# The roots of six late norms go through DRAM to reach all partitions, where TensorE transposed them before

## The chip, the cores and the metric

The kernel runs on one NeuronCore of a Trainium2 chip. The metric is the device time of one execution in microseconds (us). The program is scheduled ahead of time: each engine (TensorE = PE, VectorE = DVE, ScalarE = ACT, GpSimd = POOL, and SyncE = SP, which issues nearly all DMAs) has one fixed list of instructions, runs it in order, and waits at an instruction until what it needs is there.

## The reference

One layer over 2048 frames of 1024 features, in float32. Both sub-layers sit between two RMS norms:

```
def rms_norm(x, g):
    y = x * rsqrt(mean(x * x, axis=-1) + RMS_EPS)
    return y * g

h = rms_norm(x, g_pre_mix)
m = chunk_relpos_attention(h, w_qkv, w_o, rel_bias)      # 16 heads, 64-frame chunks, 8 chunks back
x = x + rms_norm(m, g_post_mix)
h = rms_norm(x, g_pre_ffn)
x = x + rms_norm((silu(h @ w_gate) * (h @ w_up)) @ w_down, g_post_ffn)   # 2816 hidden features
```

A norm needs one number per frame, the root 1/sqrt(mean + eps).

## The kernel before, in words

Data lie features on partitions, frames along the row: a tile of 128 partitions x 512 frames is one block of features of a half of 512 frames. Four halves make two groups (g = 0 and 1) of 1024 frames. Attention for both groups comes first, then, for each group, `gate_up(g)` and `down(g)`. Matrix products are made as three float32r matmuls of high and low parts (`products`, lines 192 to 194), 512 columns each. The feed-forward products are cut into seven products per block (Strassen's scheme): `gate_up` has 11 chunks, each of which does the products B11, B21 (into bank pair `pa`), T1 (`pc`), T2 (`pb`), B22 (`pc` again), T3 and T4 (`pb` again), 24 matmuls each. Between them DVE and ACT read the banks: line 1017 copies, 1031 and 1032 make the differences and sums `u2` and `p5` after T1 and T2, 1036 closes, 1047 makes the outputs T1 to T4, which SP stores to DRAM. T3 adds into the banks that line 1031 has to have read. Weights come by DMA into one of four `raw` buffers; ACT (line 128) rounds them to a high part and DVE (line 129) forms the low part.

The work of the norms is laid beside those products as a list of small steps, `later`. Every three matmuls one unit of credit (`tick`) is given, and a step is put into the program when its price is paid; `pause(w)` is a step that only costs w. PE's list is in the order in which this is written. The lists of the other engines and of the SP queue are put in order by a scheduler that works with estimated times, so an instruction of theirs can stand well before or after the place at which its step was written.

A late norm goes like this. `Late.sums` loads eight tiles and adds their squares into `total` (128 partitions x 512 frames, each partition with its own sums). `rstd_steps` then has `by_token`: four matmuls against a column of ones give the sums over partitions as a 128 x 4 column (frame on partition; line 275), DVE scales it (280), POOL raises it to the power -1/2 (282) into `rs`. After a pause of 6, `back` needs that root as a row, the same in every partition: `transposed` (line 302) lets PE multiply the column, repeated 128 times, with the identity, four times 128x128, and ACT (297) copies the bank over `total`. `Late.write` then loads y and the residual again, multiplies by `total` (line 1212), adds (1215) and stores.

There are four such norms: two after the mixing of group 1 during `gate_up(0)`, two after the feed-forward of group 0 during `gate_up(1)`. Besides, `blocks[1]` (the norm ahead of group 1's feed-forward) sums its two halves during `gate_up(0)`, keeps the roots as columns `hr`, and `spreads` makes two rows `row` of them; line 795 reads these when `blocks[1].all` makes the operands of `gate_up(1)`.

Of the kernel before, what the change touches and what calls it, by code (L numbers as in the profile page):

```python
# [9 lines left out]
F32 = mybir.dt.float32  # L10
# [6 lines left out]
P = 128  # L17
# [6 lines left out]
HALF = 512  # L24
# [26 lines left out]
def trunk(  # L51
# [22 lines left out]
    dram = ctx.enter_context(tc.tile_pool(name="dram", bufs=1, space=DRAM))  # L74
# [123 lines left out]
    later = deque()  # L198
# [29 lines left out]
    def pause(w):  # L228
        return [(w, lambda: None)]
# [27 lines left out]
        act.activation(sq, src, AF.Square)  # L257
        eng.tensor_tensor(total, total, sq, op=ALU.add)

    def rstd_steps(total, dst, wait=8.0, keep=None, bank=None, extra=None, then=None):  # L260

        nb = total.shape[-1] // P
        bank = bank or norm_bank
        r = {}

        def by_token():  # L270
            pt = bank("pssq")
            for b in range(nb):
                terms = [total] if extra is None else [total, extra]
                for n, t in enumerate(terms):
                    pe.matmul(  # L275
                        pt[:, 0, b : b + 1], t[:, b * P : b * P + P], ones[:, 0:1],
                        start=n == 0, stop=n == len(terms) - 1,
                    )
            m = const.tile([P, 4], F32, tag="ms", name="ms", bufs=2)
            dve.tensor_scalar(m[:, :nb], pt[:, 0, :nb], 1.0 / D, EPS, op0=ALU.mult, op1=ALU.add)  # L280
            r[0] = const.tile([P, 4], F32, tag="rs", name="rs", bufs=2) if keep is None else keep
            pool.tensor_tensor(r[0][:, :nb], m[:, :nb], neg_half.to_broadcast([P, nb]), op=ALU.pow)  # L282

        def back():
            if then is None:
                spread(r[0], dst, bank)
            else:
                then(transposed(r[0], nb, bank))

        return [(1.0, by_token)] + pause(wait) + [(1.0, back)]  # L290

    def norm_bank(name):
# [2 lines left out]
    def spread(r, dst, bank=norm_bank):  # L295

        act.activation(dst, transposed(r, dst.shape[-1] // P, bank), AF.Copy)

    def transposed(r, nb, bank):
        pt = bank("prs")  # L300
        for b in range(nb):
            pe.transpose(pt[:, b, :], r[:, b : b + 1].to_broadcast([P, P]), ident)
        return pt[:, :nb, :].rearrange("p b t -> p (b t)")

    class Prep:
# [26 lines left out]
        def rstd(self, wait=8.0, bank=None):  # L332
            return [(0.0, lambda: later.extendleft(reversed(rstd_steps(self.total, self.r, wait, bank=bank))))]
# [62 lines left out]
    class Post:  # L396
# [11 lines left out]
        def rstd(self, wait=8.0):  # L408
            return rstd_steps(self.total, self.total, wait)
# [37 lines left out]
    phase = {}  # L447
# [304 lines left out]
    class Blocks:  # L752
# [9 lines left out]
        def sums(self, w):  # L762

            steps = []
            for t in range(2):
                c = {}

                def load(k, t=t, c=c):
                    c[k] = io("sum")
                    sp.dma_start(c[k], self.src[t][:, k, :])  # L770

                def use(k, c=c):
                    if k == 0:
                        self.total = nrm_tile("total")
                    add_square(c.pop(k), self.total, k == 0)

                steps += behind(w, KT, 1, load, use)
                steps.append((3.0, lambda t=t: rstd_steps(self.total, None, keep=self.r[t])[0][1]()))
            return steps

        def spreads(self):
            self.rows = []

            def one(t):
                row = phase["fp"].tile([P, HALF], F32, tag="tot", name="row", bufs=2)
                self.rows.append(row)
                spread(self.r[t], row)

            return [(1.0, lambda t=t: one(t)) for t in range(2)]

        def column(self, dst, t, k):
            sp.dma_start(dst, self.src[t][:, k, :])

# [191 lines left out]
    def bank(name):  # L985
        return phase["psf"].tile([P, HALF], F32, tag="pd", name=name, bufs=6)
# [192 lines left out]
    class Late:  # L1179
# [17 lines left out]
            return behind(w, KT, 1, load, use)  # L1197

        def rstd(self, wait):
            return [(0.0, lambda: later.extendleft(reversed(rstd_steps(self.total, self.total, wait))))]  # L1200

        def write(self, w):
            c = {}
# [17 lines left out]
    def begin():  # L1221
# [28 lines left out]
        for k in range(KT):  # L1250
            if k % 2 == 0:
                c, here = k // 4, slice(k % 4 * 256, k % 4 * 256 + 512)
                sp.dma_start(raws[c][:, here], plan[0][:, k * 256 : k * 256 + 512])
                hi, lo = ready[0][c]
                split_part(hi[:, here], lo[:, here], raws[c][:, here])
            column(0, k, cols[0][k])
# [4 lines left out]
        for k in range(KT):  # L1261
            column(1, k, cols[1][k])
# [67 lines left out]
    def dense():  # L1330
# [57 lines left out]
        for g in range(NG):  # L1388
            i = 2 * g
            if g == 0:  # L1390
                later.extend(blocks[0].third(1.5) + pause(44.0))
                for t in range(2):
                    late = Late(y_d[t], POST_MIX, x[2 + t], x1_d[2 + t])
                    later.extend(late.sums(6.0) + late.rstd(6.0) + late.write(10.0))
                later.extend(pause(12.0) + blocks[1].sums(8.0) + blocks[1].spreads())
            else:
                for late in halves:
                    later.extend(late.sums(6.0) + late.rstd(6.0) + late.write(10.0))
# [19 lines left out]
            total, begun, last_sq, rows_ = [], set(), {}, [None, None]  # L1418
# [70 lines left out]
    blocks = [Blocks(g) for g in range(NG)]  # L1489
# [7 lines left out]

    sums = weight_sums()
    work = dense()
    spent = [0.0]  # L1500
    owed = [0.0]
# [26 lines left out]
    for g in range(NG):  # L1528
# [4 lines left out]
        due, total = [], 0.0  # L1533
# [99 lines left out]
```

## Time and profile before

| | us |
|---|---|
| median of 3 timed runs | 2411.97 (2411.55 to 2414.48) |
| the profiled execution | 2410.04 |
| its span, first to last instruction | 2408.2 |
| PE busy | 2390.0 |
| DVE busy | 1459.0 |
| ACT busy | 1030.7 |
| POOL busy | 295.0 |

The span is what lies between the first and the last instruction; 1.8 us of the profiled execution lie outside it. An engine's busy time is the time in which its records show an instruction in work; PE's are pipelined, so their ends are modelled, and the starts tell the pace. `gate_up(0)` runs from about 1062 to 1484 us, `down(0)` to about 1760, `gate_up(1)` to about 2080, `down(1)` to the end.

### The profile page before, as it was taken

To read this page: it belongs to the slowest core of one execution; us is meant where nothing else is said; L and a number is where in the kernel's file an instruction comes from. 1 tells how busy PE (TensorE), PEld (TensorE's weight loads), DVE (VectorE), ACT (ScalarE), POOL (GpSimd) and SP (SyncE) were. 2 spreads that over 40 slices of the span, in tenths; PEclk is the share of its full clock that TensorE was granted. 3 is DMA by queue.
4 is the path that set the end of the run, shared out by engine and by line. 5 is a ranking of instruction groups with operands and counts; after the bars stand their busy time and mean duration, and the time that the engine had idled before them with its cause. 6 is when DMAs were issued, how large, how long until landed. Compare 5 with 4: busy or idle time off the path is not lost.

```text
span 2408.2 us, 34848 instructions
## 1 busy us (share of the span) xinstructions
PE 2390.0 (99%) x12562; PEld 1991.2 (83%) x12562; DVE 1459.0 (61%) x2568; ACT 1030.7 (43%) x1805; POOL 295.0 (12%) x382
## 2 busy tenths in 40 slices
PE   9999999999999999999999999999999999999998
PEld 8888888789787878878888888888888888888886
DVE  6546465586555554666666665577656755555577
ACT  5344344554344443545333343365443333334454
POOL 0233332102233322210000000000000000000002
PEclk9999999999999999999999999999999999999999
DMA  7689988757988875555576663577667754457654
GB/s 220 182 215 241 256 233 222 233 178 203 228 239 228 229 182 127 158 178 194 172 260 204 229 201 123 174 229 257 214 211 244 232 172 155 141 173 236 193 192 153
DMA packets 195836, 488.41 MB, mean 203 GB/s; under 512 B 25392, under 2 KB 27456, under 8 KB 185936
## 3 DMA queue, kind: packets, MB, share of 16 engines
q1 hardware_dynamic: 190032, 451.59, 58.6%
q0 software_dynamic: 5632, 34.61, 8.5%
q8 instruction: 99, 1.62, 0.3%
q14 instruction: 73, 0.60, 0.1%
HBM read 356.54 MB, written 148.42 MB: 210 GB/s over the span
## 4 chain that ended last, share of the span: by engine, by line
PE 56%; DVE 0%; POOL 0%; issue 0%; ACT 0%; DVEq 0%
PE pd L193 6%; PE pd L192 6%; PE pd L194 6%; PE pb L192 5%; PE pb L193 5%; PE pb L194 5%; PE pa L192 3%; PE pc L192 3%; PE pa L193 3%; PE pa L194 3%; PE pc L193 3%; PE pc L194 3%; PE mm L192 1%; PE mm L193 1%; PE mm L194 1%; PE pssq L275 0%
## 5 line engine op out<-in xcount | busy, mean ns | idle before, releaser
L596 ACT ACTIVATE sc<-sc,nmax 128x640 f32<-128x640 f32 (+4 forms) x256 | 193.1, 756 | 250.8 <-DVE nmax L592 250.5
L192 PE MATMUL mm<-hb,whi 128*128 128x512 f32 x704 | 283.7, 403 | 0.5 <-ACT y L253 0.5
L194 PE MATMUL mm<-hb,wlo 128*128 128x512 f32 x704 | 276.3, 392 | 0.0
L193 PE MATMUL mm<-hb,whi 128*128 128x512 f32 x704 | 275.5, 391 | 0.0
L600 POOL TENSOR_SCALAR sc<-sc,rows 128x640 f32<-128x640 f32 (+4 forms) x256 | 191.4, 750 | 644.1 <-DVE rows L599 618.2
L592 DVE CUSTOM_DVE_ANT_0 sc<-st,bias 128x640 f32<-128x640 f32 (+4 forms) x256 | 179.4, 737 | 73.1 <-PE st L584 71.4
L192 PE MATMUL pb<-hb,whi_gu_T 128*128 128x512 f32 x528 | 206.0, 390 | 0.0
L194 PE MATMUL pb<-hb,wlo_gu_T 128*128 128x512 f32 x528 | 205.5, 389 | 0.0
L193 PE MATMUL pb<-hb,whi_gu_T 128*128 128x512 f32 x528 | 205.4, 389 | 0.0
L282 POOL TENSOR_TENSOR rs<-ms,neg_half 128x4 f32<-128x4 f32 (+1 forms) x11 | 17.0, 1547 | 1234.2 <-DVE ms L280 1234.2
L194 PEld LDWEIGHTS mm<-hb,wlo 128*128 128x128 f32 x704 | 132.1, 188 | 28.9
L192 PEld LDWEIGHTS mm<-hb,whi 128*128 128x128 f32 x704 | 132.5, 188 | 24.5 <-issue 1.6
L193 PEld LDWEIGHTS mm<-hb,whi 128*128 128x128 f32 x704 | 132.6, 188 | 21.8
L193 PE MATMUL pd<-a,whi_d_T 128*128 128x512 f32 (+1 forms) x368 | 140.0, 380 | 0.4 <-DVE a L376 0.4
L192 PE MATMUL pd<-a,whi_d_T 128*128 128x512 f32 (+1 forms) x368 | 140.1, 381 | 0.0
L194 PE MATMUL pd<-a,wlo_d_T 128*128 128x512 f32 (+1 forms) x368 | 139.7, 380 | 0.0
L583 PE MATMUL st<-k,q 128*128 128x384 f32 (+1 forms) x448 | 137.9, 329 | 0.0
L192 PE MATMUL pa<-hb,whi_gu_B 128*128 128x512 f32 x352 | 137.3, 390 | 0.0
L194 PE MATMUL pa<-hb,wlo_gu_B 128*128 128x512 f32 x352 | 137.0, 389 | 0.0
L193 PE MATMUL pa<-hb,whi_gu_B 128*128 128x512 f32 x352 | 137.0, 389 | 0.0
L129 DVE TENSOR_TENSOR wlo_gu_T<-raw,whi_gu_T 128x1024 fp32r<-128x1024 f32 x88 | 107.5, 1221 | 48.2 <-ACT whi_gu_T L128 48.0
L128 ACT ACTIVATE whi_gu_T<-raw 128x1024 fp32r<-128x1024 f32 x88 | 93.2, 1060 | 91.3 <-PE pa L193 29.0
(230 smaller groups left out, 5666.2 us busy)
## 6 DMA issues: line engine op xcount, KB each, us to landing
raw<-gu_S SPq DMA_DIRECT2D x88, 512.0 KB, 3.7
raw<-in_w_gu SPq DMA_DIRECT2D x66, 512.0 KB, 4.0
q<-stage SPq DMA_DIRECT2D x128, 256.0 KB, 5.8
y<-y SPq DMA_DIRECT2D x96, 256.0 KB, 4.3
gu_S<-in_w_gu SPq DMA_DIRECT2D x44, 512.0 KB, 6.3
raw_d<-d_S SPq DMA_DIRECT2D x88, 256.0 KB, 3.6
raw_a<-aT SPq DMA_DIRECT2D x88, 256.0 KB, 3.7
raw<-in_w_a SPq DMA_DIRECT2D x42, 512.0 KB, 6.4
```

The costliest lines, as they stand in the source:

```text
L128: act.activation(hi, raw, AF.Copy)
L129: dve.tensor_tensor(lo, raw, hi.bitcast(F32), op=ALU.subtract)
L192: pe.matmul(pt, a_hi, b_hi, start=first, stop=False, skip_group_check=go_on)
L193: pe.matmul(pt, a_hi, b_lo, start=False, stop=False, skip_group_check=go_on)
L194: pe.matmul(pt, a_lo, b_hi, start=False, stop=last, skip_group_check=go_on)
L282: pool.tensor_tensor(r[0][:, :nb], m[:, :nb], neg_half.to_broadcast([P, nb]), op=ALU.pow)
L583: pe.matmul(st[:, a:b], q[:, 2 * h, cols], kk[:, h, key], start=True, stop=False)
L592: dve.tensor_tensor_reduce(out=sc[:, :n], in0=st[:, c0 : c0 + n], in1=rev, scale=-1.0, scalar=3.0e38, op0=ALU.add, op1=ALU.min, accum_out= ...
L596: act.activation(sc[:, :n], sc[:, :n], AF.Exp, bias=nmax, scale=-1.0, accum_out=rows[:, 0:1])
L600: last_pool[0] = pool.tensor_scalar(sc[:, :n], sc[:, :n], rows[:, 1:2], 1.0, op0=ALU.mult, op1=ALU.mult)
```

## The change

For the four late norms (`Late.rstd`) and the two rows of `blocks[1]`, the step `back` is replaced by two DMAs on the SP queue. `there` writes the column of roots to a DRAM tile `row`, 4 x 128, turned by its access pattern: partition p's four numbers go to row[0, p] to row[3, p], so a contiguous run is one number of 4 bytes, 512 of them. `back` reads the 512 numbers as one row of 2 KB and gives it to all 128 partitions (a step of zero over the partitions), into `total` or `row`. Pauses of 8 stand between the two and behind the second.

```diff
+    def by_dram(r, dst, wait):
+        n_row[0] += 1
+        nb = dst.shape[-1] // P
+        row = dram.tile([4, P], F32, name=f"row_{n_row[0]}")
+        def there():
+            sp.dma_start(row.rearrange("b p -> p b"), r()[:, :nb])
+        def back():
+            t = row[0:1, 0:1]
+            sp.dma_start(dst, bass.AP(tensor=t.tensor, offset=t.offset, ap=[[0, P], [1, nb * P]]))
+        return [(1.0, there), (wait, back)] + pause(wait)
...
+        if dram_wait is not None:
+            return [(1.0, by_token)] + pause(wait) + by_dram(lambda: r[0], dst, dram_wait)
         return [(1.0, by_token)] + pause(wait) + [(1.0, back)]
...
+        def spreads_by_dram(self):
+            def one(t):
+                row = phase["fp"].tile([P, HALF], F32, tag="tot", name="row", bufs=2)
+                self.rows.append(row)
+                later.extendleft(reversed(by_dram(lambda: self.r[t], row, 8.0)))
+            self.rows = []
+            return [(4.0, lambda t=t: one(t)) for t in range(2)]
...
         def rstd(self, wait):
-            return [(0.0, lambda: later.extendleft(reversed(rstd_steps(self.total, self.total, wait))))]
+            steps = lambda: rstd_steps(self.total, self.total, wait, dram_wait=8.0)
+            return [(0.0, lambda: later.extendleft(reversed(steps())))]
...
-                later.extend(pause(12.0) + blocks[1].sums(8.0) + blocks[1].spreads())
+                later.extend(pause(12.0) + blocks[1].sums(8.0) + blocks[1].spreads_by_dram())
```

The first norms of the program and the last ones (in `down(1)`) keep the transposes. POOL's list does not change. On PE six groups of four transposes go, and four of the column sums stand later than before.

On PE, between chunk 1 and chunk 2 of `gate_up(0)` (`pb` is T4, `pa` the next B11), before:

```order
L193 MATMUL pb<-hb_23_11666,whi_gu_T_12017 128x512
L194 MATMUL pb<-hb_23_11666,wlo_gu_T_12018 128x512
L302 MATMUL prs<-ident,rs 128x128 x4
L192 MATMUL pa<-hb_17_11154,whi_gu_B_12061 128x512
L193 MATMUL pa<-hb_17_11154,whi_gu_B_12061 128x512
L194 MATMUL pa<-hb_17_11154,wlo_gu_B_12062 128x512
```

On PE, the same place after the change:

```order
L193 MATMUL pb<-hb_23_11666,whi_gu_T_12017 128x512
L194 MATMUL pb<-hb_23_11666,wlo_gu_T_12018 128x512
L192 MATMUL pa<-hb_17_11154,whi_gu_B_12061 128x512
L193 MATMUL pa<-hb_17_11154,whi_gu_B_12061 128x512
L194 MATMUL pa<-hb_17_11154,wlo_gu_B_12062 128x512
```

The two products now follow each other.

On the SP queue, the same place before (`aB`, `aT` are stores of the chunk's outputs; `raw` is a weight load):

```order
L71 DMA aB_0_137<-terms 128x512
L71 DMA raw_12276<-in_w_gu 128x1024
L71 DMA aT_0_138<-terms 128x512
L71 DMA aT_0_136<-T_12146 128x512
L71 DMA aB_0_134<-terms 128x512
```

And after the change (`row_12141` is the DRAM tile of the first norm):

```order
L71 DMA aB_0_137<-terms 128x512
L71 DMA row_12141<-rs 128x4x1
L71 DMA raw_12269<-in_w_gu 128x1024
L71 DMA aT_0_138<-terms 128x512
L71 DMA aT_0_136<-T_12147 128x512
L71 DMA total<-row_12141 128x512
L71 DMA aB_0_134<-terms 128x512
```

The other five kept their order. The read of the row has to wait for the end of its write, and the store of `aB_0_134` and all that follows stand behind it.

On DVE, after the change, the first readers of that row (line 1241, which was line 1212) stand between the last output of chunk 1 and the weights of chunk 2, with the readers of T2's bank (line 1059, which was 1031) at the end of the piece:

```order
L1075 TENSOR_TENSOR T_12195<-terms,T_12147 128x512
L1241 SCALAR_TENSOR_TENSOR y<-y,gt,total 128x512 x2
L1244 TENSOR_TENSOR y<-res,y 128x512 x2
L129 TENSOR_TENSOR wlo_gu_B_12236<-raw_12200,whi_gu_B_12235 128x1024
L1035 TENSOR_TENSOR b_12251<-b_12251,pa 128x512
L129 TENSOR_TENSOR wlo_gu_T_12272<-raw_12233,whi_gu_T_12271 128x1024
L1241 SCALAR_TENSOR_TENSOR y<-y,gt,total 128x512
L1244 TENSOR_TENSOR y<-res,y 128x512
L1060 TENSOR_TENSOR terms<-terms 128x512
L129 TENSOR_TENSOR wlo_gu_T_12306<-raw_12269,whi_gu_T_12305 128x1024
L1060 TENSOR_TENSOR terms<-terms 128x512
L1059 TENSOR_TENSOR terms<-terms,pb 128x512 x2
```

Before, the first reader stood at the same place, alone.

On DVE, chunk 9 of `gate_up(0)` after the change, where the second row of `blocks[1]` (`row`) is first read only a few rows behind the scaling of its sums (`ms`):

```order
L1075 TENSOR_TENSOR T_14216<-terms,T_14175 128x512
L297 TENSOR_SCALAR ms<-pssq 128x4
L129 TENSOR_TENSOR wlo_gu_B_14267<-raw_14221,whi_gu_B_14266 128x1024
L823 SCALAR_TENSOR_TENSOR b_14837<-b_14837,gt,row 128x512
L823 SCALAR_TENSOR_TENSOR b_14838<-b_14838,gt,row 128x512
L1035 TENSOR_TENSOR b_14282<-b_14282,pa 128x512
L129 TENSOR_TENSOR wlo_gu_T_14304<-raw_14264,whi_gu_T_14303 128x1024
L1060 TENSOR_TENSOR terms<-terms 128x512
L129 TENSOR_TENSOR wlo_gu_T_14338<-raw_14301,whi_gu_T_14337 128x1024
L1060 TENSOR_TENSOR terms<-terms 128x512
L1059 TENSOR_TENSOR terms<-terms,pb 128x512 x2
```

Before, these readers stood in chunk 8, behind the two groups of transposes of that place.

## Rows read from the trace of the kernel before

**Rows 1.** The page: busy time by engine, and the chain that ended last.

```profile
PE 2390.0 (99%) x12562; PEld 1991.2 (83%) x12562; DVE 1459.0 (61%) x2568; ACT 1030.7 (43%) x1805; POOL 295.0 (12%) x382
...
PE 56%; DVE 0%; POOL 0%; issue 0%; ACT 0%; DVEq 0%
```

**Rows 2.** Windows: stretch, its length, busy us of each engine, clock, DMA.

```profile
core 0: us, PE busy (x) PEld busy (x) DVE busy (x) ACT busy (x) POOL busy (x), PEclk, DMA share, GB/s
1062.00:1460.00 398.00, 398.00 (x1780) 330.06 (x1779) 265.44 (x356) 158.92 (x219) 5.74 (x4) 1.00 0.64 210
1460.00:1765.00 305.00, 305.00 (x1346) 252.24 (x1346) 197.31 (x298) 139.94 (x233) 0.00 (x0) 1.00 0.63 203
1765.00:1900.00 135.00, 135.00 (x608) 111.83 (x607) 89.71 (x121) 51.39 (x70) 3.38 (x2) 1.00 0.72 234
1900.00:2280.00 380.00, 380.00 (x1678) 314.59 (x1677) 208.64 (x282) 134.63 (x194) 0.00 (x0) 1.00 0.56 183
```

**Rows 3.** The chain in order of time: start, us, what; the transposes.

```profile
1202.99 0.44 PE prs L302 x4
...
1454.66 0.50 PE prs L302 x4
...
1893.13 0.44 PE prs L302 x4
```

**Rows 4.** Timeline of PE, chunk 1 to 2: start, duration, instruction.

```profile
1197.16 0.95 PE L275 MATMUL pssq<-ones,total 128*128 128x1 f32 x8
...
1202.83 0.60 PE L302 MATMUL prs<-ident,rs 128*128 128x128 f32 x4
1203.18 0.48 PE L192 MATMUL pa<-hb,whi_gu_B 128*128 128x512 f32 x1
1203.50 0.39 PE L193 MATMUL pa<-hb,whi_gu_B 128*128 128x512 f32 x1
...
1214.18 0.39 PE L192 MATMUL pc<-hb,whi_gu_T 128*128 128x512 f32 x1
...
1219.62 0.39 PE L192 MATMUL pb<-hb,whi_gu_T 128*128 128x512 f32 x1
...
1230.50 0.39 PE L192 MATMUL pb<-hb,whi_gu_T 128*128 128x512 f32 x1
```

**Rows 5.** The tile `prs`: count, min/median/max ns.

```profile
L302 PE MATMUL prs<-ident,rs x40: 270/272/323, 493.2 to 2399.1; 128*128 128x128 f32 x40
```

**Rows 6.** Timelines of DVE, POOL and ACT around the first late norm.

```profile
1198.39 1.42 POOL L282 TENSOR_TENSOR rs<-ms,neg_half 128x4 f32<-128x4 f32 x1 [147.97 <-DVE ms L280]
...
1205.57 0.69 DVE L1047 TENSOR_TENSOR T<-terms,T 128x512 f32<-128x512 f32 x1
1208.18 0.75 DVE L1212 SCALAR_TENSOR_TENSOR y<-y,gt,total 128x512 f32<-128x512 f32 x1 [1.93 <-issue]
...
1215.29 1.23 DVE L129 TENSOR_TENSOR wlo_gu_T<-raw,whi_gu_T 128x1024 fp32r<-128x1024 f32 x1 [0.16 <-ACT whi_gu_T L128]
...
1219.64 1.06 ACT L128 ACTIVATE whi_gu_T<-raw 128x1024 fp32r<-128x1024 f32 x1 [1.94 <-PE pc L193]
```

**Rows 7.** Timeline of SP: when it issued, same place.

```profile
1198.95 0.32 SPq L71 DMA_DIRECT2D aB<-terms  x1
1200.08 0.33 SPq L71 DMA_DIRECT2D raw<-in_w_gu  x1
...
1201.29 0.32 SPq L71 DMA_DIRECT2D aT<-T  x1
```

**Rows 8.** DMA issues: count, KB each, median us to landing.

```profile
y<-y SPq DMA_DIRECT2D x96, 256.0 KB, 4.3
...
aB<-terms SPq DMA_DIRECT2D x43, 256.0 KB, 2.0
...
vh<-vh SPq DMA_DIRECT2D x4, 512.0 KB, 7.6
...
ext_d<-ext SPq DMA_DIRECT2D x1, 48.0 KB, 2.6
```

More of the change, by code (lines that the diff above doesn't have):

```diff
@@ L258, in add_square, with rstd_steps @@
         eng.tensor_tensor(total, total, sq, op=ALU.add)
-    def rstd_steps(total, dst, wait=8.0, keep=None, bank=None, extra=None, then=None):
+    n_row = [0]
+    def by_dram(r, dst, wait):
[8 more added lines that the diff above has]
+        return [(1.0, there), (wait, back)] + pause(wait)
+    def rstd_steps(total, dst, wait=8.0, keep=None, bank=None, extra=None, then=None, dram_wait=None):
         nb = total.shape[-1] // P
```

## The prediction

> **What bounds the kernel now.** I read the page first, then stretches, then PE's own timeline around the six places. PE is busy 2390.0 of 2408.2 us and the chain that ended last is PE's almost alone [rows 1]. What matters more is the stretch in which the change works: from 1062 us, shortly before `gate_up(0)`, to 2280 us, well into `down(1)`, PE is busy in every microsecond of 398, 305, 135 and 380, at the full clock of 1.00 [rows 2]. So PE waits for nobody there. DVE has 265.44 of 398 us of work in the first stretch, ACT 158.92, the DMA engines 0.64 of theirs. Two things follow. A microsecond taken off PE's list there is a microsecond off the end, since everything later hangs on PE's place in its list. And work taken from ACT, DVE or POOL, or given to the DMA queues, counts only if it makes PE wait.
>
> **What the change takes off PE.** Six groups of four transposes. One group's cost is to be read from starts. The transposes start at 1202.83 and the second matmul behind them at 1203.50 [rows 4]. From 1202.83 to 1203.50 is 0.67 us, in which one ordinary matmul also went; 24 of these take from 1214.18 to 1219.62, so 0.227 each. The group costs 0.67 - 0.23 = 0.44 us, and the chain books 0.44 for it as well [rows 3]. It books 0.44 for five of the six groups (the first and the last are shown) and 0.50 for the second of the pair at 1454.66, where PE waited a little for the root. The sum is 5 x 0.44 + 0.50 = 2.70 us. The four matmuls of column sums per norm stay, only later.
>
> ACT loses six copies of a bank. Since PE never waited for ACT in the stretch, I price that at nothing; the cover is PE's full stretch.
>
> **What the change adds.** Twelve DMAs on SP, no instruction on another engine. None of them can hold PE directly. They can hold it in two ways: through DVE, which waits at the first reader of the row with its later work behind it, and through SP, which waits at the read of the row until the write has landed, with stores and weight loads behind it.
>
> The durations are in no row, since no DMA here writes runs of 4 bytes or reads one row into all partitions. For the write, the nearest rows are stores to DRAM: 2.0 us for the 256 KB of `aB`, 2.6 for the small `ext_d`, and 7.6 for the slowest sort, `vh`, DRAM to DRAM [rows 8]. I take 2.6, the small one, and keep 2.0 and 7.6. For the read, the 256 KB load `y` takes 4.3; I take that, the same size, and keep the same 2.0 and 7.6 as ends. The way there and back is then 6.9 us, between 4.0 and 15.2.
>
> How much is covered? First norm: the root is ready at 1198.39 + 1.42 = 1199.81 [rows 6]. SP has just issued `aB` (1198.95) and issues the next load at 1200.08 [rows 7], so the write goes out at about 1199.9. SP then issues the load and two stores, the last of which was issued at 1201.29. The row lands at about 1199.9 + 6.9 = 1206.8. DVE reaches its first reader when T4's output is done, at 1205.57 + 0.69 = 1206.26: a wait of half a microsecond, and 8.8 at the upper end. Before, this reader ran at 1208.18 anyway.
>
> What is late next? Of what is queued behind, the first that PE needs is the read of T2's bank, without which T3 can't start at 1230.50 [rows 4]. By the order of the changed kernel, in front of it and with it stand three multiplications (0.75 each), three additions of y, the product of the halves, two sums and that read (seven at 0.69) and three low parts of weights (1.23 each): 2.25 + 4.83 + 3.69 = 10.8 us. The row has to be there at 1219.7; the way there and back may take 19.8 us before PE waits. Its upper end is 15.2.
>
> The fifth norm (first of `gate_up(1)`) stands like the first. The second and the sixth are easier: their sums come three matmuls into B22, so the write goes out some 9 us earlier against the chunk's end. Of the pair of rows, the first is written in T3 of chunk 7 and read a chunk later. The second is the tightest. Its sums come six matmuls (1.4 us) into chunk 9, and at the first norm it took from 1197.16 [rows 4] to 1199.81 from the start of the sums to the root, 2.65, so the write goes out 4.0 us into the chunk; T3 starts 27.3 in (1203.18 to 1230.50), and DVE has between the first reader and the read of T2's bank 2 x 0.75 + 4 x 0.69 + 2 x 1.23 = 6.7 us to do. That leaves 27.3 - 6.7 - 4.0 = 16.6 us for a way that takes 6.9, at most 15.2. Hidden as well, with 1.4 us to spare at the worst.
>
> SP: at the first norm it is held from about 1201.7 until the write has landed, 1202.5 by the value taken, 1207.5 at the upper end. Behind it stand stores and loads of weights. A load issued at 1200.08 goes into a buffer whose turn at ACT comes four splits later, at 1219.64 [rows 6, 7], and PE uses that weight three products later still. Some 15 us of cover against at most 6 of delay: nothing.
>
> The steps behind each root come 16 units of credit later, the two rows of `blocks[1]` 40 units later in all. Priced by the steps' weights the list of `gate_up(0)` grows from 476 to 548 of the 616 units that its 77 products of 8 give, so nothing is left over to be done in a heap at its end.
>
> **The sum.** 2410.04 - 2.70 = 2407.3 us for an execution like the profiled one, a span of 2405.5. The profiled execution lies 1.9 us below the median of the timed runs. Taken off the median, 2411.97 - 2.7 = 2409.3 us, 0.11% less. A difference of 0.2% (4.8 us) is about what a measurement of this kernel can tell from none, so my forecast is a real gain that counts as no change.
>
> **Rivals.**
>
> *The transposes cost more than their gap.* Each has a record of 272 ns [rows 5], and 24 x 0.272 = 6.5 us would give 2405.5, faster by 0.27%. Against it: matmuls overlap, and the starts in rows 4 tell 0.44 for four. Chance 0.06.
>
> *The gain is eaten.* DVE's and SP's lists stand in another order over both `gate_up` stages, and a reader of y that meets a late load in front of a bank's closing would hold PE; the closings of T3 have 2.7 us (12 matmuls) before T4 needs the bank. One or two such waits give back the 2.7 us: about 2412. For it: the order is made from estimates. Against it: the same loads and readers stood in such places before and PE never waited [rows 2]. Chance 0.12; four of them or more, beyond 2416.8, 0.04.
>
> *The way through DRAM is long: the slower side.* It decides from 16.6 us on, where the tightest place starts to hold PE; from 19.8 on the first and fifth norm do too, from about 29 the second and sixth, each microsecond one for one. Suppose that a run costs the same whatever its length. The 256 KB load of `y` moves 128 rows of 2 KB in 4.3 us [rows 8]; 512 runs would then take four times that, 17.2, and with the read 21.5 us. The places lose 4.9 and 2 x 1.7, together 8.3, and the time is 2409.3 + 8.3 = 2417.6 us. For it: 512 runs of 4 bytes, which nothing in the trace shows. Against it: the volume is 2 KB, and at the pace of a store, 2.0 us for 128 rows, the same rule gives 8.0 + 4.3 = 12.3, still hidden. Chance 0.06.
> [...]
>
> *The change does nothing on PE* can't be: the transposes are gone from its list.
>
> **How the numbers follow.** The forecast, all hidden, has 0.72, and its own range is 2407.5 to 2411 (the spread of the runs before around 2409.3). The gap priced by records has 0.06, the eaten gain 0.12, four waits or more 0.04, the long way 0.06. The range from 2406.0 to 2413.0 holds the forecast with its spread and the eaten gain, and leaves out most of the first rival and the slow ones. Faster by over 0.2% (below 2407.1): the first rival and the lucky edge of the forecast, 0.11. Slower: 0.10. Within: 0.79.
>
> **What would show it.** In the profile after: no transposes between 1062 and 2300 us; PE busy in every microsecond of the same stretches; the last stretch begins about 2.7 us earlier. The row for the write of `row` lands in 2 to 8 us, the read in 2 to 7. DVE waits at line 1241 or 823 for a DMA, up to 8 us at a place, without PE waiting for line 1059 or 129. SP waits for the write at the read, six times. I am wrong if PE waits for DVE's line 1059, 1064 or 129 in `gate_up`, or if the write takes over 12 us.

## The result: slower by 0.17%, where a gain of 0.11% was forecast

The changed kernel takes 2416.16 us (median of 22 runs, 2413.52 to 2418.43) against 2411.97 us (22 runs, 2409.85 to 2416.2): ratio 1.0017, 95% interval 1.0011 to 1.0023. That is 4.2 us more where 2.7 us less were forecast, and above the range, which ended at 2413.0. The profiled execution took 2416.78 us, its span is 2415.0.

The page of the kernel after says that TensorE lost its 24 transposes [rows 1: x12562], and the windows of [rows 2], taken again, that it no longer works in every microsecond:

```profile
PE 2391.1 (99%) x12538; PEld 1989.7 (82%) x12538; DVE 1456.3 (60%) x2568; ACT 1027.3 (43%) x1799; POOL 294.7 (12%) x382
```

```profile
core 0: us, PE busy (x) PEld busy (x) DVE busy (x) ACT busy (x) POOL busy (x), PEclk, DMA share, GB/s
1062.00:1460.00 398.00, 396.54 (x1759) 327.47 (x1758) 261.79 (x352) 155.91 (x214) 4.36 (x3) 1.00 0.69 212
...
1900.00:2280.00 380.00, 376.61 (x1650) 311.27 (x1651) 207.34 (x281) 131.75 (x189) 1.96 (x1) 0.99 0.57 182
```

TensorE is idle for 1.5 us in the first stretch and 3.4 in the last. The waits of that whole stretch (engine and line that waited, what it waited for; us in total, times, longest) name the readers of a bank that VectorE was late with, line 1064 (which was 1036) above all:

```profile
PE pb L192 <- DVE terms L1064: 4.5, 3, 3.4
PE pa L192 <- ACT terms L1045: 0.4, 1, 0.4
PE pb L192 <- DVE terms L1059: 0.3, 1, 0.3
...
SPq L71 <- DMA row<-rs: 35.7, 4, 10.4
SPq L71 <- POOL rs L299: 17.8, 4, 6.7
SPq L71 <- DMA row<-hr: 9.3, 1, 9.3
...
DVE y L1241 <- DMA y<-y: 39.5, 15, 6.5
DVE y L1241 <- DMA total<-row: 20.2, 2, 10.6
...
DVE b L823 <- DMA row<-row: 10.2, 1, 10.2
```

SyncE stood 45 us at the reads of the row, VectorE waited for loads of y for 39.5 us (before: 20.9 in the whole program), and for the row itself up to 10.6. The reason stands in the DMA issues of the kernel after (KB each, median us to landing), which answer to [rows 8]:

```profile
y<-y SPq DMA_DIRECT2D x96, 256.0 KB, 4.2
...
total<-row SPq DMA_DIRECT2D x4, 256.0 KB, 5.8
row<-row SPq DMA_DIRECT2D x2, 256.0 KB, 5.1
row<-rs SPq DMA_DIRECT2D x4, 2.0 KB, 10.4
row<-hr SPq DMA_DIRECT2D x2, 2.0 KB, 9.6
```

The write of 2 KB takes 10 us, more than any DMA that the prediction compared it with; the read takes 5 to 6.

Where does TensorE pay? The weights that its matmuls read tell the stages of the kernel before: `gate_up(0)` runs from 1126 to 1550 us, `down(0)` to 1760 and `gate_up(1)` to 2182, later than the section on the profile before has them. From the starts of the same matmuls in both traces: TensorE is 0.41 us behind before the first norm, gains what each group of transposes cost (2.9 us in all), loses 1.6 us at the first norm and 1.2 at the second, and stands 0.49 behind ahead of the sixth. Behind the sixth it is 6.74 behind, to the end. There the SP queue, VectorE and TensorE read as follows (start, duration, instruction; in brackets the idle time before it and what ended it):

```profile
1902.42 0.37 SPq L71 DMA_DIRECT2D row<-rs  x1
1902.84 0.51 SPq L71 DMA_DIRECT2D raw<-gu_S  x1
1912.30 0.32 SPq L71 DMA_DIRECT2D total<-row  x1
...
1917.98 0.32 SPq L71 DMA_DIRECT2D y<-y  x1
...
1940.28 0.40 SPq L71 DMA_DIRECT2D y<-y  x1
```

```profile
1925.60 0.75 DVE L1241 SCALAR_TENSOR_TENSOR y<-y,gt,total 128x512 f32<-128x512 f32 x1 [6.48 <-DMA y<-y]
...
1946.14 0.75 DVE L1241 SCALAR_TENSOR_TENSOR y<-y,gt,total 128x512 f32<-128x512 f32 x1 [3.38 <-DMA y<-y]
1946.81 0.68 DVE L1064 TENSOR_TENSOR terms<-pc,terms 128x512 f32<-128x512 f32 x1
...
1951.15 0.68 DVE L1064 TENSOR_TENSOR terms<-pb,terms 128x512 f32<-128x512 f32 x1
```

```profile
1948.11 0.39 PE L194 MATMUL pb<-hb,wlo_gu_T 128*128 128x512 f32 x1
1951.88 0.79 PE L192 MATMUL pb<-hb,whi_gu_T 128*128 128x512 f32 x1 [3.39 <-DVE terms L1064]
1952.47 0.63 PE L193 MATMUL pb<-hb,whi_gu_T 128*128 128x512 f32 x1
```

SyncE issues nothing from 1902.84 to 1912.30, then a heap; the loads of y come late one after the other, VectorE waits 14 us for three of them (4.16 for the one not shown), and TensorE waits 3.39 us for the reader of the bank `pb`, last in that block. The next matmuls start 0.43 apart (1952.47, 1952.90 and so on) instead of 0.23. Windows of the same place show the granted clock meanwhile (PEclk, ahead of the DMA share):

```profile
1948.00:1951.80 3.80, 0.49 (x3) 0.07 (x1) 3.70 (x6) 1.11 (x2) 0.00 (x0) 0.83 0.63 202
1951.80:1957.10 5.30, 5.22 (x12) 4.13 (x13) 4.67 (x8) 1.58 (x2) 0.00 (x0) 0.50 0.69 204
```

After the idle 3.4 us the granted clock is 0.50 for 5.3 us, in which 12 matmuls run; at 0.2 us each that costs 2.4 us more. This one place cost 6.2 of the 9.2 us that were given back.

### The profile page after: what moved, and what is told of

It is laid out like the page before. It is cut to its first block, busy times and chain, and to the rows that moved or that the text cites. A ratio compares the mean times of both kernels' runs of the same rounds, so it can differ in the third digit from the quotient of the medians.

```text
span 2415.0 us, 34816 instructions
## 1 busy us (share of the span) xinstructions
PE 2391.1 (99%) x12538; PEld 1989.7 (82%) x12538; DVE 1456.3 (60%) x2568; ACT 1027.3 (43%) x1799; POOL 294.7 (12%) x382
## 4 chain that ended last, share of the span: by engine, by line
PE 32%; issue 20%; DMA 3%; DVE 1%; POOL 0%; SPq 0%; ACT 0%; DVEq 0%; POOLq 0%
PE pd L193 3%; PE pd L192 3%; PE pd L194 3%; PE pb L192 3%; PE pb L193 3%; PE pb L194 3%; PE pa L193 2%; PE pa L194 2%; PE pa L192 2%; PE pc L192 2%; PE pc L193 2%; PE pc L194 2%; PE mm L192 1%; PE mm L194 1%; PE mm L193 1%
```

## The experiments

Three theories stood at first. **H**: SyncE stands behind the read until the write has landed, so loads of y, res and sums go out late or in a heap. **R**: the row itself reaches VectorE late. **O**: the other order of the lists alone costs the time. **Q** came with the first runs: the write holds up the transfers queued behind it. The medians of the kernel before were 2410.8 to 2411.9 us in the five sets of runs. The ratio compares the runs of both kernels in a set and is not the quotient of two medians. Two further kernels, six_writes and six_writes_moved, ran once each, for their traces.

| run | median us | ratio, 95% interval |
|---|---|---|
| read_on_pool | 2422.52 | 1.0045, 1.0031 to 1.0059 |
| both_on_pool | 2448.54 | 1.0155, 1.0141 to 1.0169 |
| dmas_beside | 2415.24 | 1.0020, 1.0008 to 1.0032 |
| write_beside | 2415.67 | 1.0014, 1.0005 to 1.0022 |
| runs_16b, and again | 2408.87, 2408.35 | 0.9989, 0.9981 to 0.9998; 0.9988, 0.9979 to 0.9997 |
| one_column | 2425.14 | 1.0055, 1.0041 to 1.0068 |
| late_read | 2430.76 | 1.0078, 1.0065 to 1.0092 |
| pair_only | 2418.46 | 1.0027, 1.0017 to 1.0038 |
| norms_only | 2415.73 | 1.0014, 1.0005 to 1.0023 |
| runs_apart | 2408.17 | 0.9986, 0.9977 to 0.9994 |
| runs_16b_in_order | 2414.19 | 1.0007, 0.9998 to 1.0015 |
| act_orders | 2413.21 | 1.0005, 0.9996 to 1.0014 |
| token_fours | 2413.93 | 1.0008, 0.9999 to 1.0017 |
| order_in_sum | 2409.90 | 0.9989, 0.9979 to 0.9998 |

**Shorter write, same lists.** `row` becomes 128 x 4, so that each partition's four roots are one run of 16 bytes.

```diff
-        row = dram.tile([4, P], F32, name=f"row_{n_row[0]}")
+        row = dram.tile([P, 4], F32, name=f"row_{n_row[0]}")
...
-            sp.dma_start(row.rearrange("b p -> p b"), r()[:, :nb])
+            sp.dma_start(row[:, :nb], r()[:, :nb])
```

> The row in DRAM is 128 x 4, so the write goes in 128 runs of 16 bytes where it went in 512 of 4; the row then has the roots in another order (this part of the computation is changed, its volume and its instructions are not). If the write's 10 us come from its 512 runs, it lands in 2.5 to 5 us, SP is held at most 3 us at a place, and H and R both give 2409 to 2412 us. If they come from something else (the queue in front of it, the landing in DRAM), it takes 8 to 10 us again and the time is 2415 to 2418 us. Theory O: 2414 to 2418 us with a write of any length.

> The kernel of the run with 128 runs of 16 B once more, on this chip: the loads and the time before the changed stretch differ by some us from profile to profile, so its gain is to be seen twice. If it is the change's own, the ratio is again 0.998 to 0.9995; if it was chance of one chip, it is 1.000 to 1.001. As before, the roots of the four blocks lie interleaved in the row, so the numbers in it are in another order.

The issues and the waits of the first of the two:

```profile
row<-rs SPq DMA_DIRECT2D x4, 2.0 KB, 2.0
...
SPq L71 <- POOL rs L299: 17.8, 4, 6.7
SPq L71 <- DMA row<-hr: 3.5, 1, 3.5
SPq L71 <- DMA row<-rs: 2.9, 3, 1.9
...
DVE y L1241 <- DMA total<-row: 2.6, 2, 1.6
PE pa L192 <- ACT terms L1045: 1.3, 1, 1.3
```

The predicted gain is there, on two chips, with the lists in the changed kernel's order and the same transposes gone. So O falls, and SyncE's 17.8 us of waiting for roots harm nobody. All of the loss hangs on the 10 us of the write. TensorE's one wait here, 1.3 us for line 1045 at the start of `gate_up(1)`, stands nowhere near a norm; most of the runs below have it too.

**What the long write does.** SyncE's wait is taken away by issuing the read, then both, from GpSimd (both: two DMAs of 256 runs for the write).

```diff
-            sp.dma_start(dst, bass.AP(tensor=t.tensor, offset=t.offset, ap=[[0, P], [1, nb * P]]))
+            pool.dma_start(dst, bass.AP(tensor=t.tensor, offset=t.offset, ap=[[0, P], [1, nb * P]]))
```

> The write of the roots stays on SP, the read of the row is issued from POOL, so that POOL and not SP waits for the write to land. Theory H (SP is held behind the read until the write has landed, so the loads of y and residual behind it come late, DVE waits for them in front of the closings of T3, and PE waits for these): the SP queue's 35.7 + 9.3 us of waiting for the write go, PE's 4.5 us of waits on line 1064 fall under 1 us, 2409 to 2412 us. Theory R (the row itself comes late at DVE's reader): the row comes no earlier, 2415 to 2418 us. Theory O (the new order of the lists alone makes PE wait): 2414 to 2418 us.

> [...] SP waits neither for the root (17.8 us in four waits after the change) nor for the write. Theory H: 2408.5 to 2411 us, PE's waits on line 1064 and 1059 under 0.5 us. Theory R: the row comes as late or later, 2415 to 2420 us. Theory O: 2414 to 2418 us.

SyncE no longer waits for a write in the first, and the kernel is slower still. In the fifth norm the order now puts a reader of the row ahead of an addition (line 1035), for which ScalarE's copy of a bank (line 1045) has to wait. VectorE and TensorE of that run:

```profile
1816.42 0.75 DVE L1241 SCALAR_TENSOR_TENSOR y<-y,gt,total 128x512 f32<-128x512 f32 x1 [11.92 <-DMA total<-row]
1817.09 0.68 DVE L1035 TENSOR_TENSOR terms<-terms 128x512 f32<-128x512 f32 x1
```

```profile
1818.51 0.80 PE L192 MATMUL pa<-hb,whi_gu_B 128*128 128x512 f32 x1 [6.59 <-ACT terms L1045]
```

So R can hold TensorE as well: a way of some 16 us (the write went out at 1800.71, the reader ran at 1816.42) is more than what the order leaves there. At the second and the sixth norm, though, read_on_pool has every list in the changed kernel's order but for the read itself, and the write is as slow (10.9 and 9.2 us). There TensorE loses nothing and 0.6 us, where the changed kernel lost 1.2 and 6.2; the one wait left is this:

```profile
1961.29 0.50 PE L192 MATMUL pb<-hb,whi_gu_T 128*128 128x512 f32 x1 [0.26 <-DVE terms L1064]
```

At the sixth norm the first load of y goes out at the same place of the chunk in both runs, but lands in 4.8 us and not in 7.5; no heap of held transfers stands ahead of it. So at these two places, 7.4 of the 9.2 us, the loss comes by H.

With both DMAs on GpSimd the two halves of the write take 8 to 11 us each, one behind the other, and VectorE waits up to 20.1 us for a row.

Then the transposes stay and feed the work, and the DMAs stand beside them, unread by VectorE: write and a read of 32 numbers, or the write alone.

```diff
-            return [(1.0, by_token)] + pause(wait) + by_dram(lambda: r[0], dst, dram_wait)
+            return [(1.0, by_token)] + pause(wait) + [(1.0, back)] + by_dram(lambda: r[0], spare[0], dram_wait)
```

> The transposes are back as before the change, and the two DMAs of each of the six places are added on SP; the read brings 32 numbers into a spare tile that nobody reads. Theory H: SP is held for the write as in the changed kernel, so PE waits as there without the 2.8 us gained: 2415 to 2421 us, PE waits for line 1064. Theory R: nobody waits for the row, 2411 to 2413 us. Theory O: between 2412 and 2416 us.

> The transposes stay and feed the work as before; the six writes of 512 runs of 4 B to DRAM are added from SyncE, and nothing reads them back, so SyncE never waits for a write to land. Theory H (the loss comes from SyncE standing behind the read until the write lands, so that loads of y, res and sum are issued late): no loss, 2411 to 2412 us, no TensorE wait in the stretch. Theory Q (the 512 runs keep the transfers queued behind them from landing): the loads issued just behind a write still land 5 to 10 us late, with TensorE waits of some us at one or two places, 2413 to 2417 us. SyncE still waits up to 7 us for the root at two of the writes under both; if that alone is the cause, waits in front of TensorE stand only at norms 2 and 6.

The seven runs of dmas_beside lie between 2411.0 and 2421.0 us, and the trace is that of the slowest. In it TensorE waits once, 4.1 us, behind ScalarE, which stands for a load of `sum`. That load, the second of the two here, went out at 1430.36 and was still under way when a write was issued at 1434.89:

```profile
1429.88 0.91 SPq L71 DMA_DIRECT2D sum<-x  x2
1434.89 0.37 SPq L71 DMA_DIRECT2D row<-hr  x1
```

```profile
1444.95 0.63 ACT L257 ACTIVATE sq<-sum 128x512 f32<-128x512 f32 x1 [9.98 <-DMA sum<-x]
```

The load lands 14.6 us after its issue, its twin before it took 4.4, and the write lands 0.8 us later than the load. SyncE has no part in this, as the load was issued 4.5 us ahead of the write. Not every transfer under way is held: in the changed kernel a load of `sum` issued 0.7 us ahead of a write took 9.8 us, one issued 2.8 us ahead 4.7. Weight loads issued about a microsecond or less behind such a write took 10.3 to 13.3 us to land, in the changed kernel, read_on_pool, norms_only, one_column and late_read and at the first norm of write_beside; behind the short writes of runs_16b, runs_apart and the others below they took 4.4 to 5.4. At the first norm, the load `raw<-in_w_gu` before the change, and after it:

```profile
DMA to landing us min/median/max: 3.9/3.9/3.9
```

```profile
DMA to landing us min/median/max: 12.9/12.9/12.9
```

That is Q. In the changed kernel the next weight load behind five of the six writes took 9.6 to 13.1 us (behind the other none went out until the write had landed), and the two loads of `sum` above, 9.8 and 14.6 us, were ahead of theirs. In write_beside the late loads had cover: TensorE's one wait of size, 1.9 us at a group of sums, comes with the same 1.89 in six_writes and six_writes_moved below, whose pair writes land in 1.4 to 7.5 us. It belongs to the order of that kernel's lists, not to the write, so this run does not tell H from Q as it was meant to.

**Part of the change, and a later read.** The pair alone, the four norms alone, and 17 units of credit between write and read in place of 8. The edits of the last two:

```diff
-                later.extend(pause(12.0) + blocks[1].sums(8.0) + blocks[1].spreads_by_dram())
+                later.extend(pause(12.0) + blocks[1].sums(8.0) + blocks[1].spreads())
...
-        return [(1.0, there), (wait, back)] + pause(wait)
+        return [(1.0, there)] + pause(16.0) + [(1.0, back)] + pause(wait)
```

> Only the four norms in the residual go by DRAM, the pair keeps its transposes. Under H and Q alike the loss of the changed kernel lies at these norms, above all at the first, second and sixth: as the changed kernel and 0.9 us on top for the transposes of the pair, 2416 to 2418 us, ratio 1.0015 to 1.0025. If the loss hung on the pair, 2411 to 2412 us.

> Only the pair of block norms goes by DRAM, the four other norms keep their transposes. The pair showed no TensorE wait in the trace of the changed kernel and lost its 0.94 us of transposes: 2410.8 to 2411.5 us, the ratio 0.9995 to 1.000. If loads behind the two writes are late all the same (theory Q), 2412 to 2414 us.

> As the changed kernel, but some 16 us of planned work stand between the write's issue and the read's, so SyncE no longer waits for the write to land (0 to 2 us in place of 10.4). H: the SyncE wait is gone and with it the late y and res loads, but the row itself comes some 10 us later; if it is still covered, 2409 to 2411 us. Q: loads behind a write stay late, 2413 to 2417. R (the row itself reaches its VectorE reader late): waits for the row at VectorE grow from 10 to some 15 us and more, and TensorE waits where a bank closing stands behind such a reader: 2413 to 2420 us.

norms_only comes out just under its forecast. pair_only is a miss for every theory as I had put them: in the changed kernel the pair cost nothing, alone it costs more than the whole change. VectorE in chunk 9 of that run:

```profile
1459.79 0.69 DVE L1064 TENSOR_TENSOR terms<-pc,terms 128x512 f32<-128x512 f32 x1 [0.63 <-PE pc L194]
1467.59 1.42 DVE L823 SCALAR_TENSOR_TENSOR b<-b,gt,row 128x512 f32<-128x512 f32 x2 [7.11 <-DMA row<-row]
1468.92 0.68 DVE L1064 TENSOR_TENSOR terms<-pc,terms 128x512 f32<-128x512 f32 x1
```

The write goes out at 1454.59, SyncE stands 8.3 us, the read follows at 1463.33 and lands at 1467.5, and the order has this row's reader between two closings (line 1064); TensorE waits 4.9 us, and the granted clock is 0.86 on the mean from 1467.50 to 1473.00. The way was 13 us here, under the 16.6 that the prediction allowed this place, whose order was another. Late_read is a miss too, above all its cases: SyncE still stands up to 8.7 us at a read, VectorE waits for the row at all four norms (34.8 us together), and TensorE waits five times for line 1045, 7.2 us together. The cover is what the order of that one kernel leaves, and pair_only and late_read have quite other orders.

**Why the write is slow.** First one column alone: 128 runs of 4 bytes. The read repeats it four times, so the rows hold one block's numbers.

```diff
-            sp.dma_start(row.rearrange("b p -> p b"), r()[:, :nb])
+            sp.dma_start(row[0:1].rearrange("b p -> p b"), r()[:, 0:1])
```

> Only the root column of the first 128 tokens is written (128 runs of 4 B in place of 512) and the read repeats it for all four blocks, so the numbers in the rows of the other three blocks are those of the first; the transposes are gone. If the time of a write goes with the number of its runs, it lands like the 128 runs of 16 B did: 2.0 to 2.6 us, and the kernel takes 2408.5 to 2410 us. If runs under 16 B have a price of their own per run, the write stays at 5 to 10 us and the kernel at 2412 to 2417 us. Theories H, Q and R give the same under each.

A quarter of the runs takes 8.3 us. The time is not the number of runs, and as the read now takes 10.3 us (four pieces of 512 bytes per partition), the kernel's time fits neither case. Then six forms, each at two places, beside the transposes:

```diff
+        shape = ([P, 4, 16], [P, 16], [1, P], [P, 16], [4, P], [P, 4])[n - 1]
...
+            if n == 1:
+                sp.dma_start(row[:, :, 0:1], r().rearrange("p (b o) -> p b o", o=1))
+            elif n == 2:
+                sp.dma_start(row[:, 0:1], r()[:, 0:1])
```

> The transposes stay; the six writes stand beside them and nobody reads them, each in a form of its own: at the first norm 512 runs of 4 B, 64 B apart in DRAM; at the second 128 of 4 B, 64 B apart; in the pair 128 of 4 B side by side, then 128 of 16 B, 64 B apart; at the fifth 512 of 4 B side by side (the change's own); at the sixth 128 of 16 B side by side. If the price goes with the number of runs: about 10, 2.5, 2.5, 2.5, 10 and 2 us. If with runs under 16 B: 8 to 10 wherever a run has 4 B, 2 for both of 16 B. If with neighbours sharing a stretch of DRAM: 2 to 4 us for those that lie apart, 8 and 10 for the 4 B side by side.

> The same six forms, each three places on: at the first norm 128 runs of 16 B, 64 B apart; at the second 512 of 4 B side by side; in the pair 128 of 16 B side by side, then 512 of 4 B, 64 B apart; at the fifth 128 of 4 B, 64 B apart; at the sixth 128 of 4 B side by side. Each form takes the time that it took at its other place, within 1.5 us, if the form sets it; a place where any form is slow points to the transfers around it instead.

The second norm's write and the pair's two, as the DMA issues of six_writes list them (128 runs of 4 B apart; side by side; 128 of 16 B apart), and then all forms:

```profile
row<-rs SPq DMA_DIRECT2D x1, 0.5 KB, 1.9
row<-hr SPq DMA_DIRECT2D x1, 0.5 KB, 7.5
row<-hr SPq DMA_DIRECT2D x1, 2.0 KB, 1.4
```

| form | landing, us, at its two places |
|---|---|
| 512 runs of 4 B, side by side (the change) | 8.9, 8.2 |
| 512 runs of 4 B, 64 B apart | 2.9, 2.9 |
| 128 runs of 4 B, side by side | 7.5, 7.9 |
| 128 runs of 4 B, 64 B apart | 1.9, 1.6 |
| 128 runs of 16 B, side by side | 1.8, 2.8 |
| 128 runs of 16 B, 64 B apart | 1.4, 2.5 |

Neither count nor size alone gives these times: 512 runs of 4 bytes take 8.9 and 8.2 us side by side and 2.9 set apart, and the same 2 KB side by side in runs of 16 bytes 1.8 and 2.8. The two slow forms are those whose 4-byte runs lie next to each other in DRAM, 7.5 to 8.9 us against 1.4 to 2.9 for the other four. Last, the changed kernel whole with its 512 runs 64 bytes apart; the read takes the first 2 KB of that tile, filled once before, so the rows hold other numbers.

```diff
+            shared.append(dram.tile([P, 4, 16], F32, name="row"))
+            sp.dma_start(shared[0].rearrange("p b o -> p (b o)"), ident[:, :64])
...
-            sp.dma_start(row.rearrange("b p -> p b"), r()[:, :nb])
+            sp.dma_start(row[:, :, 0:1], r()[:, :nb].rearrange("p (b o) -> p b o", o=1))
```

> The changed kernel with its 512 runs of 4 B, which now lie 64 B apart in DRAM, in a tile that is filled once ahead of the first norm; the read takes the first 2 KB of it, so the rows hold other numbers than the roots. If the kernel's loss comes from the time until the write lands (10 us), it is gone: the write lands in 2.9 us, SyncE is held 2 to 4 us, and the time is that of the run with 128 runs of 16 B, 2408 to 2410 us. If 512 small runs cost the kernel something whatever they take to land, as late loads behind them, 2412 to 2416 us.

```profile
total<-row SPq DMA_DIRECT2D x4, 256.0 KB, 4.3
...
row<-rs SPq DMA_DIRECT2D x4, 2.0 KB, 2.9
```

As many small runs as in the change, and the whole gain. That settles it for this kernel, whose lists keep their order here: the loss comes from the slow write, and not from the number of its runs.

**The gain with the rows in order.** The 16-byte form leaves the frames interleaved. Four ways to mend it: VectorE's readers take the row through a view with a step of 16 bytes (runs_16b_in_order, where the rows of `blocks[0]`, which still come from transposes, are read by the same view and so are out of order); ScalarE copies the row into order; the sums' matmuls take every fourth frame as a column; or the last addition of squares writes its sum in that order. The edits of the last two:

```diff
-                        pt[:, 0, b : b + 1], t[:, b * P : b * P + P], ones[:, 0:1],
+                        t.rearrange("p (t b) -> p b t", b=nb)[:, b] if fours else t[:, b * P : b * P + P],
...
+        view = lambda t: t.rearrange("p (t b) -> p t b", b=4)
+        eng.tensor_tensor(fours.rearrange("p (b t) -> p t b", b=4), view(total), view(sq), op=ALU.add)
```

> The write of 128 runs of 16 B, each partition its four roots side by side, and the readers of the row take it through a view that puts the tokens in their places, so the whole computation stands. If VectorE's reads with a stride of 16 B cost nothing here (0.75 us for a 128x512 multiplication before), the time is that of the run with 128 runs: 2408 to 2410 us, the ratio 0.9985 to 0.9995. If the stride doubles those 48 multiplications to 1.5 us, VectorE is busier by 36 us spread over the stretch, mostly hidden: 2408 to 2412 us.

> The write of 128 runs of 16 B, the row read into a scratch tile, and one ScalarE copy of 128x512 puts the tokens in order; VectorE reads plain rows again and the computation stands whole. Six ScalarE copies take the place of the six copies out of PSUM of the kernel before, about 0.6 to 1.1 us each, and the copy stands in ScalarE's order where it may wait for the row. If the loss of the other ordered version is its 72 VectorE operations of 1.14 us in place of 0.75 us, this one keeps the gain: 2408.5 to 2410.5 us, ratio 0.9985 to 0.9995. If ScalarE waits for the row in front of a square or a bank's copy, TensorE waits behind it: 2411 to 2415 us.

> The write of 128 runs of 16 B, and the sums' own matmuls take every fourth token as a column (the stationary operand read with a stride of 16 B), so that each partition holds the roots of four tokens that follow one another and the row lands in DRAM in order: the computation stands whole and no instruction is added. If the strided weight loads of the 24 one-column products cost TensorE nothing, the time is that of the run with 128 runs: 2408 to 2409.5 us, ratio 0.998 to 0.9993. If each of them costs as much as a pass of 0.23 us more, 24 of them give 5.4 us back: 2413 to 2415 us.

> The write of 128 runs of 16 B, and the last of the eight additions of squares of each of the six norms writes its sum with every four tokens brought together (a VectorE addition with strides, into the tile whose square was added last), so the sums' matmuls give each partition four tokens that follow one another, from contiguous weight loads, and the computation stands whole. Price: six VectorE additions of about 1.1 us in place of 0.69 us, each just ahead of its group of sums. If that is all, 2408 to 2410 us, ratio 0.998 to 0.9995. If the late sum holds TensorE at the group, which stands behind it in order, up to 0.4 us each: 2411 to 2412 us.

The instructions that leave their neighbours, in the four runs in that order; the first three read with a step of 16 bytes, the last one writes with a step of 512:

```profile
L824 DVE SCALAR_TENSOR_TENSOR b<-b,gt,row 128x512 f32<-128x512 f32 x36 | 40.0, 1146 | 12.2 <-DMA b<-x 7.2 <-DMA row<-row 4.1 <-ACT row L316 0.7
```

```profile
L278 ACT ACTIVATE total<-mixed x4: 1107/1108/1115, 1210.9 to 1923.0; 128x512 f32<-128x512 f32 x4
```

```profile
L292 PEld LDWEIGHTS pssq<-ones,total x48: 307/329/329, 1196.8 to 1903.1; 128*128 128x128 f32 x48
```

```profile
L262 DVE TENSOR_TENSOR y<-total,sq x4: 1107/1108/1112, 1198.7 to 1890.8; 128x512 f32<-128x512 f32 x4
```

Every one costs 1.5 to 1.9 times what it costs on neighbours (0.75, 0.60, 0.192 and 0.69 us). In the first there are 72 such operations and not the 48 of the expectation, as the norm of `blocks[0]` uses the same view. TensorE's longest wait, 2.4 us at 1096 us, lies at that norm, so this version lost more than the row's order asks for; of two waits of 1.2 us, one is behind a closing at 1952 us and one at the start of `gate_up(1)`, where runs_16b waits too. In the second, ScalarE waited 9.9 us for the rows; TensorE waits 0.4 us behind it, 1.3 for a late sum and 1.4 at the start of `gate_up(1)`. In the third the one wait of TensorE (1.5 us) is again that one; the group of weight loads takes 0.84 us more per norm than before, against 0.47 won. The intervals of these three take in 1: each gave the gain back, and none is shown to be slower than the kernel before. The fourth puts the step into six additions of 1.1 us that TensorE never waits for: it has no wait in the whole stretch, and the ratio, 0.9989, is below 1 with the rows in order.

## Why the prediction was wrong

**Its first part held.** TensorE was full, and the transposes' price was 0.44 to 0.50 us a group: in the changed kernel TensorE gains 0.46 to 0.5 us at each place where a group has gone and nothing new waits. The forecast itself, 0.11% less, is what runs_16b, runs_apart and order_in_sum measured (0.9986 to 0.9989). The read was well sized: 5.1 to 5.8 us for 4.3.

**The step that failed is the write's duration.** "I take 2.6, the small one", with 7.6 as the upper bound; it took 9.6 to 10.4. The rows it was bounded by are DMAs with long runs, and none tells how writes of 4 bytes next to each other go. The rival for this, that a run costs the same whatever its length, had 8.0 us for the write at a store's pace, or 17.2; but its rule is wrong too, as 128 such runs take 7.5 to 8.3 and 512 set apart 2.9.

**The second failed step is SyncE.** "Some 15 us of cover against at most 6 of delay: nothing" counted the weight loads alone. Behind the held SyncE also stand the loads of y, res and sum for VectorE and ScalarE, whose readers stand in order ahead of the readers of banks: without SyncE's standing, in read_on_pool, the second and sixth norm lost 0.6 us and not 7.4. And loads that SyncE has already issued land late as well, 12.9 for 3.9 us, which the prediction had not thought of. The weight loads did have the cover that it gave them.

**The covers for the row at VectorE** (19.8 and about 29 us, 16.6 for the pair) were near the mark for the changed kernel's own order: a way of some 16 us made VectorE wait up to 10.6 us at the first and fifth norm and 10.2 at the pair, and TensorE at most at the first, which cost 1.6 us. There the next load of y (issued 1220.46) stood on SyncE behind the store of the first y (1218.34), which waited for the reader of the row. They are no property of the place, as read_on_pool and pair_only show. So the slower side came, but by the mechanism of "the gain is eaten", a reader of y that meets a late load in front of a bank's closing. It went deeper than the one or two waits of that rival (2412 us), as behind the wait of 3.4 us the granted clock was 0.50 and 2.4 us more were lost, which the prediction had not counted. That the write itself brought this about, through SyncE and the loads behind it, was seen by neither rival.

**What stays open.** At the second and sixth norm read_on_pool tells H from the rest. How the 1.6 us of the first norm divide between H, Q and R is open: all come from the same 10 us, and no run parts them there in the same order. Why neighbouring 4-byte runs take so long to land is not shown either.

## What to carry to other kernels

A small DMA is not always a short one (here 2 KB took 10.4 us in 4-byte runs side by side, 2.0 in runs of 16 bytes): look at the runs and at where they lie in DRAM, and let each partition write its numbers as one run, even if the order has to be made elsewhere. When a queue is to be held or its transfers slowed, count all that stands behind it on that queue, the loads of the element-wise work too, and follow their readers in each engine's order up to the next reader of a bank. A change of order is best put into the instruction that has the fewest repetitions and the most cover: six additions cost TensorE nothing here, 48 weight loads ate the gain.

## What the runs showed of the hardware

512 runs of 4 bytes side by side took 8.2 to 11.3 us to land, 64 bytes apart 2.5 to 3.8. Weight loads issued about a microsecond or less behind a slow write landed in 10.3 to 13.3 us, behind a short one in 4.4 to 5.4; a load issued 4.5 us ahead of a slow write took 14.6, its twin before it 4.4. After a wait of TensorE of 3.4 us the granted clock was 0.50 for the next 5.3 us, 12 matmuls at 0.43 us instead of 0.23, and the place cost 6.2 us in all. With a step of 16 bytes in what they read, a multiplication of 128x512 on VectorE took 1.15 us for 0.75, a copy of 128x512 on ScalarE 1.11 for 0.60 and a weight load of TensorE 0.329 for 0.192, 1.5 to 1.9 times as long; an addition of 128x512 on VectorE that writes with a step of 512 bytes took 1.11 for 0.69.
